# FFN1's first pair: another order of its operands, copies and second-half products

## The chip, the cores and the metric

The kernel runs on one core of a Trainium2 chip. Its time is the device time of one execution in microseconds (us). Three runs of the kernel before took 1942.91, 1944.48 and 1946.78 us; their median is 1944.48.

The engines are called as in the profile: PE is TensorE (matrix products; PEld its weight loads), DVE is VectorE, ACT is ScalarE, POOL is GpSimd, and SP is the engine that issues most DMA transfers. Each has its own queue of instructions; they meet at semaphores.

## What is computed

One layer of a decoder over 1048 tokens (16 meta tokens, 1024 of a prompt, 8 of samples), width 1024, in float32. The layer has a half-step FFN, a mixer with two kinds of recurrent heads, and a second half-step FFN:

```
def rmsnorm(x, w):
    xf = x.astype(jnp.float32)
    y = xf * lax.rsqrt(jnp.mean(xf * xf, axis=-1, keepdims=True) + EPS)
    return (y * w.astype(jnp.float32)).astype(x.dtype)

def swiglu(x, wg, wu, wd):
    return (jax.nn.silu(x @ wg) * (x @ wu)) @ wd
...
    h = h + 0.5 * swiglu(rmsnorm(h, n1), w1g, w1u, w1d)
...
    h = h + mix
    h = h + 0.5 * swiglu(rmsnorm(h, n2), w2g, w2u, w2d)
```

The change lies in the first line of the layer, in the first 60 of some 1940 us: the start of `x @ wg` and `x @ wu` of FFN1, whose hidden width is 2816.

## The kernel before

**Products.** The activations stand transposed: features on the 128 partitions, tokens along the row. The tokens are cut into two halves of 524 (c = 0 and 1) and each half into two quarters of 262 (Q). For each block of 128 hidden columns f, `pair` makes gate and up values together by a scheme with seven products in place of eight: the weights are seen as a 2 x 2 matrix (gate or up, first or second 512 features), the activations of a half as another (first or second 512 features, first or second quarter). Operands 1, 7, 2 and 3 (activations) and 1, 7, 4 and 2 (weights) are plain blocks, the others are sums and differences of them: for the activations 5 = 7 - 1, 6 = 3 - 5, 7 becomes 3 - 7, and 4 = 2 - 6. Product p multiplies weight operand p by activation operand p. Products 2, 3 and 4 are added into the PSUM banks of 1, 5 and 7.

**Two parts.** Float32 operands are split in a high part (a cast on ACT, `cast` at L348 for activations, `hi` at L464 for weights) and a low part (the difference, on DVE, `low` at L354 and `lo` at L468). Sums of activations are made on DVE at L343, sums of weights at L460. `mm3` (L163 to L165) makes each product out of three matmuls: high by high, high by low part of the activations, low part of the weights by high. A product over 512 features is 12 matmuls of 262 columns; its first needs the casts, its second the activations' low part, its third the weights' low part.

**Order by hand.** An FFN is one list of steps, `Steps`; a step is a product and what is done after it (`post`). `S.before(i, fn)` puts other work ahead of step i. The queues of PE, DVE, ACT and SP follow the order of the code (`manual_schedule`), so the lists of `before(...)` in `first1` are these engines' queues, read per engine.

**The first pair.** For f = 0 the two halves are multiplied one after the other, since the input is still arriving. Steps 0 to 5 are the first half's products in the order that `first1` returns (1, 2, 5, 6, 7, 3), steps 6 to 11 the second half's in the same order, steps 12 and 13 operand 4 of the first and of the second half. Step 14 begins the next pair, f = 1, whose own weights are planned by `Left.plan` from step 3 on (loads at steps 3 and 4, sums at 10 to 12, the first cast at 11, its low part at 12). In `first1`, `o` is the first half's set of operands, `e` the second half's, `w` the weights. So "e.low 6" is the low part of the second half's operand 6, "o.sum_4" the first half's sum 4, "w.lo 4" the low part of weight operand 4. Ahead of step 0 the first half is transposed and operands 1 and 2 are made.

**The input.** The second half's tokens come in by `place_k`: for each of the 8 blocks k of 128 features, PE makes four transposes (L1191) into one PSUM bank, and ACT takes from it two scaled copies (L1193, one per quarter, times the norm's weight) into the operands' blocks and two raw copies (L1194) into blocks that SP stores to DRAM (`x.store`, L1216) for the residual. Blocks 0 to 3 are the first 512 features (operands 1 and 7), 4 to 7 the second (2 and 3). `tail` places the last 12 tokens, with a multiply on DVE (L1178) and raw copies on ACT. `x.square` (L1210) squares the raw input for the norm's root, which is needed only at step 18. The operands and raw blocks share 30 SBUF buffers called "u"; four PSUM banks ("mis") serve the transposes, and two of them are held by product 7 and operand 4 of each half.

**After a product.** After product 1 ACT copies its bank to z (L676), and product 2 may write into that bank only then; after product 2 ACT copies the sum out (L680). After products 6, 7, 3 and 4 DVE adds into SBUF (L678 and L685, L687, L691, L705); what belongs to product 5 waits for 6.

Of the kernel before, what the change touches and what calls it, by code (L numbers as in the profile page):

```python
# [17 lines left out]
P = 128  # L18
# [10 lines left out]
Q = T // 4  # L29
# [38 lines left out]
class Core:  # L68
# [49 lines left out]
    def raw(self, w=512):  # L118
        t = self.tmp.tile([P, 512], F32, tag="r", name=self.uid("r"), bufs=8)
        return t[:, :w]  # L120
# [530 lines left out]
def pair(K, S, wg, wu, f, ops, spread, hid, late_r, first=None, inner=None):  # L651
# [70 lines left out]
    if inner:  # L722
# [34 lines left out]
        e = len(S.steps)  # L757
# [12 lines left out]
    late = {}  # L770
# [9 lines left out]

    order = first(S, left)
    unit = Unit(K, left.w, [o.op for o in ops], 4, post_first)
    for ps_ in (order[:6], order[6:]):
        for c in range(2):
            for p in ps_:
                unit.step(S, p, c, (c,), True)
    cs = slice(0, 2)
    for i, (fn, *args) in enumerate(((silu, 0, cs), (silu, 1, cs), (times_r, "u0", 0, cs), (product_, 0, cs), (times_r, "u1", 1, cs), (product_, 1, cs))):
# [342 lines left out]
class Input:  # L1131
# [51 lines left out]

        return scaled, raw

    def place_k(self, k):

        K = self.K
        ps = K.psm()
        for i in range(4):  # L1190
            K.nc.tensor.transpose(ps[:, i * P : i * P + P], self.x[5 + i][:, k * P : k * P + P], K.ident)  # L1191
        for q, c0, c1 in ((2, 0, Q), (3, Q, 4 * P)):
            K.nc.scalar.activation(self.block(k // 4, q)[:, k % 4, : c1 - c0], ps[:, c0:c1], AF.Identity, scale=self.wcol[:, k : k + 1])  # L1193
            K.nc.scalar.copy(self.raw_block(k // 4, q)[:, k % 4, : c1 - c0], ps[:, c0:c1])  # L1194

    def block(self, b, q):
        o = self.ops[q // 2]
# [877 lines left out]
def body(ctx, tc, a, o):  # L2075
    nc = tc.nc
    K = Core(ctx, tc)
# [6 lines left out]
    x = Input(K, a, wn1, ops, spread)  # L2084

    def before(S, i, *fns):
        for fn in fns:
            S.before(i, (lambda fn=fn: fn[0](*fn[1:])))

    def first1(S, w):  # L2090
        o, e = ops
        x.load(0, 1, 2)
        K.keep_clock(14)
        w.load(1)
        x.load(3, 4)
        for p in (2, 7, 4):
            w.load(p)
        x.load(*range(5, 10))
        nc.scalar.preload_act_table_set("sqrt_and_others")
        columns1()  # L2100
        for i in range(2):
            scaled, raw = x.place(i)
            K.keep_clock(4)
            for fn in (scaled, raw):
                fn(0)
                fn(1)
        w.hi(1)
        scaled, raw2 = x.place(2)
        K.keep_clock(4)
        scaled(0)  # L2110
        o.cast(1)
        scaled(1)
        raw2(0)
        raw2(1)
        scaled, raw3 = x.place(3)
        K.keep_clock(4)
        scaled(0)
        o.low(1)
        scaled(1)
        w.lo(1)  # L2120
        w.hi(2)
        o.cast(2)
        scaled, raw4 = x.place(4)
        K.keep_clock(4)
        scaled(0)
        scaled(1)
        raw3(0)
        raw3(1)
        raw4(0)
        raw4(1)  # L2130
        x.square(4)
        o.low(2)
        w.lo(2)
        o.sum_(5)

        def tail():
            scaled, raw = x.place(9)
            for fn in (scaled, raw):
                fn(0)
                fn(1)  # L2140

        before(S, 1, (o.cast, 5), (w.sum_, 5), (w.hi, 5), (o.sum_, 6), (x.store, 0), (columns,), (x.place_k, 0))
        before(S, 2, (o.low, 5), (o.cast, 6), (w.lo, 5), (w.sum_, 6), (w.hi, 6), (x.place_k, 1))
        before(S, 3, (o.low, 6), (o.sum_, 7), (w.lo, 6), (o.cast, 7), (w.sum_, 7), (w.sum_, 3), (w.hi, 7), (x.place_k, 2))
        before(S, 4, (o.low, 7), (w.lo, 7), (o.cast, 3), (w.hi, 3), (x.place_k, 3), (tail,))
        before(S, 5, (o.low, 3), (w.lo, 3), (e.cast, 1), (e.sum_, 5), (x.store, 1, (0,)), (x.place_k, 4), (x.place_k, 5))
        before(S, 6, (e.low, 1), (e.cast, 5), (o.sum_, 4), (x.place_k, 6), (x.place_k, 7))
        before(S, 7, (e.cast, 2), (e.low, 5), (e.low, 2), (e.sum_, 6), (x.store, 1, (1,)), (o.cast, 4), (e.cast, 6))
        before(S, 8, (o.low, 4), (e.sum_, 7), (e.low, 6), (e.cast, 7))
        before(S, 9, (e.sum_, 4), (e.low, 7), (e.cast, 3), (x.square, 9))  # L2150
        before(S, 10, (e.low, 3), (e.cast, 4), (w.hi, 4), (w.lo, 4), (x.square, 0), (x.square, 1))
        before(S, 11, (e.low, 4), (x.square, 2))
        for i, n in enumerate((3, 5, 6, 7, 8)):
            before(S, 12 + i, (x.square, n))
        before(S, 18, (x.rms,))
        before(S, 22, *((x.spread_r, q) for q in range(4)))
        return 1, 2, 5, 6, 7, 3, 4

    def from1(o):
        return x.d[o * P : (o + 1) * P, :]  # L2160
# [1 line left out]
    def after1(S, h, e3, e0, e1):  # L2162
# [33 lines left out]
        return nm.add  # L2196

    ffn(K, a["w_ffn1_gate"][0], a["w_ffn1_up"][0], a["w_ffn1_down"][0], ops, spread, from1, first1, after1, 26)

    constants_mix(K, a)  # L2200
# [15 lines left out]
    order = "q0 f0 v0 g0 q1 f1 v1 g1 z0 q2 f2 v2 g2 q3 f3 v3 z1 g3".split()  # L2216
    raw = ("q0", "f0", "g0", "q1", "g3")
# [3 lines left out]
    with K.tc.manual_schedule(engines={mybir.EngineType.PE}):  # L2221
# [33 lines left out]
        late = late_norms(K, pieces, lambda: us[3]["g"], fill)  # L2255
# [48 lines left out]
    def first2(S, w):  # L2304
        o, e = ops2
        for p in (1, 7, 4, 2):
            w.load(p)
        o.scaled(h, wn2, (1, 7))
        o.cast(1)
        o.sum_(5)  # L2310
        o.scaled(h, wn2, (2, 3))
        o.cast(5)
        o.low(1)
        o.cast(2)
        o.sum_(6)
        o.low(5)
        o.cast(6)
        o.low(2)
        o.sum_(7)
        o.cast(7)  # L2320
        o.low(6)
        o.sum_(4)
        o.cast(3)
        o.low(7)
        o.cast(4)
        o.low(3)
        o.low(4)
        for p in (5, 6, 7, 3):
            w.sum_(p)
        w.split(1)  # L2330
        w.split(5)
        e.scaled(h, wn2, (1, 7))
        e.cast(1)
        e.sum_(5)
        e.low(1)
        e.cast(5)
        w.split(6)
        e.low(5)
        e.scaled(h, wn2, (2,), (0, 1))
        w.split(2)  # L2340
        e.scaled(h, wn2, (2,), (2,))
        before(S, 1, (e.scaled, h, wn2, (2,), (3,)), (w.hi, 7), (e.scaled, h, wn2, (3,), (0, 1)), (w.lo, 7))
        before(S, 2, (w.hi, 3), (e.scaled, h, wn2, (3,), (2, 3)), (e.cast, 2))
        before(S, 3, (w.lo, 3), (e.sum_, 6), (e.low, 2), (nf2.begin_half, 1))
        before(S, 4, (e.cast, 6), (e.sum_, 7))
        before(S, 5, (e.low, 6), (e.cast, 7))
        before(S, 6, (e.low, 7), (e.sum_, 4))
        before(S, 7, (e.cast, 3))
        before(S, 8, (e.cast, 4))
        before(S, 9, (e.low, 3), (w.hi, 4))  # L2350
        before(S, 10, (w.lo, 4), (e.low, 4), (keep2, 1))
        before(S, 15, (nf2.finish, (1, 1)))
        return 1, 5, 6, 2, 7, 3, 4

    def after3(S, h, e3, e0, e1):
        nf = []
# [15 lines left out]
        return None  # L2372

    ffn(K, a["w_ffn2_gate"][0], a["w_ffn2_up"][0], a["w_ffn2_down"][0], ops2, spread2, lambda o: hd2[o], first2, after3, 14)


# [35 lines left out]
```

## Time and profile before

| | us |
|---|---|
| runs (median of three) | 1944.48 |
| the profiled execution | 1946.32 |
| its span, first to last instruction | 1944.5 |
| busy in the span: DVE | 1535.0 |
| busy in the span: ACT | 847.1 |
| busy in the span: POOL | 92.3 |

The mean granted clock of TensorE over the span is 0.995 of full speed. A row of the order in time reads: start (us from the start of the span), length, engine, line, operation, out <- in with partitions x columns and types, count, and in square brackets the idle time of that engine just before, with the work that ended it. A row of the groups by line reads: line, engine, operation, out <- in, shapes, count, then busy time in us and mean ns of one, then idle time before them and what ended most of it. A row of stretches gives from:to, its length, then the busy time of PE, PEld, DVE, ACT and POOL with the number of instructions, the granted clock of TensorE (1 is full), the mean busy share of the 16 DMA engines, and GB/s. Neighbouring instructions of a kind that run without a gap are merged in one row. A result is finished a little after the next instruction of its engine has started, so a queue's pace is read from start to start and a dependence from the end.

### The profile page before, as it was taken

To read this page: it belongs to the slowest core of one execution; us is meant where nothing else is said; L and a number is where in the kernel's file an instruction comes from. 1 tells how busy PE (TensorE), PEld (TensorE's weight loads), DVE (VectorE), ACT (ScalarE), POOL (GpSimd) and SP (SyncE) were. 2 spreads that over 40 slices of the span, in tenths; PEclk is the share of its full clock that TensorE was granted. 3 is DMA by queue.
4 is the path that set the end of the run, shared out by engine and by line. 5 is a ranking of instruction groups with operands and counts; after the bars stand their busy time and mean duration, and the time that the engine had idled before them with its cause. 6 is when DMAs were issued, how large, how long until landed. Compare 5 with 4: busy or idle time off the path is not lost.

```text
span 1944.5 us, 41083 instructions
## 1 busy us (share of the span) xinstructions
PE 1912.5 (98%) x16571; PEld 1881.1 (97%) x16571; DVE 1535.0 (79%) x2802; ACT 847.1 (44%) x1639; POOL 92.3 (5%) x155
## 2 busy tenths in 40 slices
PE   7999999999999999999999999999999999999998
PEld 6999999999999999999999989999999999999998
DVE  7788888888788877576765657898888888878965
ACT  7623232233533644476543545752232333354353
POOL 4000000000000410000000001200000000000000
PEclk9999999999999999999999999999999999999999
DMA  7233233335978551231642354233233333587862
GB/s 223 77 89 110 90 103 105 95 104 163 274 230 264 161 162 44 60 101 29 183 131 66 104 182 143 72 100 114 83 109 94 108 100 109 161 239 238 277 186 78
DMA packets 324646, 260.59 MB, mean 134 GB/s; under 512 B 17824, under 2 KB 299680, under 8 KB 324448
## 3 DMA queue, kind: packets, MB, share of 16 engines
q1 hardware_dynamic: 324216, 257.92, 43.7%
q8 instruction: 131, 2.15, 0.5%
q14 instruction: 59, 0.48, 0.1%
q0 software_dynamic: 224, 0.04, 0.0%
q10 hardware_dynamic: 16, 0.00, 0.0%
HBM read 192.90 MB, written 65.07 MB: 133 GB/s over the span
## 4 chain that ended last, share of the span: by engine, by line
PE 92%; DVE 4%; DMA 1%; issue 1%; ACT 1%; SPq 0%; DVEq 0%; POOL 0%; ACTq 0%; POOLq 0%
PE acc L163 27%; PE acc L165 27%; PE acc L164 27%; PE mis L163 2%; PE mis L165 2%; PE mis L164 2%; DMA s<-in_x_prompt_dram 1%; PE mis L1809 1%; PE mis L1457 0%; PE mis L1880 0%; PE mis L1453 0%; DVE u L354 0%; PE mis L1785 0%; DVE t L303 0%; PE mis L1448 0%
## 5 line engine op out<-in xcount | busy, mean ns | idle before, releaser
L163 PE MATMUL acc<-u,ws 128*128 128x258 f32 (+4 forms) x4226 | 1235.1, 293 | 3.0 <-ACT u L348 1.4
L164 PE MATMUL acc<-u,ws 128*128 128x258 f32 (+4 forms) x4226 | 1224.4, 290 | 3.6 <-DVE u L354 3.3
L165 PE MATMUL acc<-u,ws 128*128 128x258 f32 (+4 forms) x4226 | 1224.9, 290 | 2.9 <-DVE ws L468 2.7
L164 PEld LDWEIGHTS acc<-u,ws 128*128 128x128 f32 x4226 | 801.1, 190 | 7.4 <-DVE u L354 4.4
L163 PEld LDWEIGHTS acc<-u,ws 128*128 128x128 f32 x4226 | 799.5, 189 | 6.4 <-issue 1.7
L165 PEld LDWEIGHTS acc<-u,ws 128*128 128x128 f32 x4226 | 798.1, 189 | 4.4 <-DVE ws L468 4.0
L468 DVE TENSOR_TENSOR ws<-r,ws 128x512 fp32r<-128x512 f32 x276 | 190.3, 690 | 74.6 <-ACT ws L464 74.5
L464 ACT CAST ws<-r 128x512 fp32r<-128x512 f32 x276 | 160.0, 614 | 13.1 <-ACT ws L464 7.8
L460 DVE TENSOR_TENSOR r<-r,r 128x512 f32<-128x512 f32 x176 | 121.5, 692 | 2.8 <-DMA r<-in_w_ffn_up_dram 1.3
L683 ACT ACTIVATE t<-t 128x516 f32<-128x516 f32 (+1 forms) x41 | 26.2, 639 | 210.8 <-DVE t L671 210.8
L714 ACT ACTIVATE t<-t 128x524 f32<-128x524 f32 (+1 forms) x47 | 30.0, 639 | 197.9 <-DVE t L671 197.9
L851 DVE TENSOR_TENSOR u<-u,u 128x1048 fp32r<-128x1048 f32 (+3 forms) x84 | 97.1, 1157 | 5.5 <-ACT u L847 5.5
L671 DVE TENSOR_TENSOR t<-t,u 128x524 f32<-128x524 f32 (+1 forms) x135 | 93.1, 697 | 2.8
L232 POOL TENSOR_TENSOR t<-t,t 128x262 f32<-128x262 f32 (+1 forms) x56 | 54.7, 986 | 798.7 <-ACT t L231 795.4
L158 DVE TENSOR_TENSOR ws<-r,ws 128x512 fp32r<-128x512 f32 x88 | 60.8, 703 | 36.8 <-ACT ws L157 36.6
L908 ACT CAST ws<-u 128x512 fp32r<-128x512 f32 (+1 forms) x72 | 42.1, 585 | 102.0 <-DVE u L903 96.4
L847 ACT CAST u<-u 128x1048 fp32r<-128x1048 f32 (+3 forms) x84 | 82.8, 988 | 0.0
L908 ACT CAST ws<-r 128x512 fp32r<-128x512 f32 (+1 forms) x84 | 47.9, 582 | 71.6 <-DVE r L903 38.4
L937 DVE SCALAR_TENSOR_TENSOR s<-acc,s 128x524 f32<-128x524 f32 (+3 forms) x86 | 53.8, 649 | 29.4 <-PE acc L165 29.1
L913 DVE TENSOR_TENSOR ws<-r,ws 128x512 fp32r<-128x512 f32 (+1 forms) x84 | 57.5, 694 | 24.0 <-ACT ws L908 23.9
L157 ACT CAST ws<-r 128x512 fp32r<-128x512 f32 x88 | 54.0, 618 | 39.7 <-PE acc L165 34.0
L913 DVE TENSOR_TENSOR ws<-u,ws 128x512 fp32r<-128x512 f32 (+1 forms) x72 | 46.8, 650 | 26.5 <-ACT ws L908 26.5
(444 smaller groups left out, 2327.5 us busy)
## 6 DMA issues: line engine op xcount, KB each, us to landing
r<-in_w_ffn_down_dram SPq DMA_DIRECT2D x128, 256.0 KB
hd<-s SPq DMA_DIRECT2D x93, 258.0 KB
r<-in_w_ffn_gate_dram SPq DMA_DIRECT2D x88, 256.0 KB
r<-in_w_ffn_up_dram SPq DMA_DIRECT2D x88, 256.0 KB
hd<-s SPq DMA_DIRECT2D x77, 262.0 KB
u<-hd SPq DMA_DIRECT2D x36, 516.0 KB
u<-hd SPq DMA_DIRECT2D x28, 524.0 KB
r<-in_w_in_dram SPq DMA_DIRECT2D x56, 256.0 KB
```

The lines of the kernel that those rows point to most:

```text
L158: self.nc.vector.tensor_sub(lo, src, hi.bitcast(F32))
L163: mm(ps, whi, xhi, start=first, stop=False, skip_group_check=more)
L164: mm(ps, whi, xlo, start=False, stop=False, skip_group_check=more)
L165: mm(ps, wlo, xhi, start=False, stop=last, skip_group_check=more)
L460: self.K.nc.vector.tensor_tensor(self.raw[p], self.raw[x], self.raw[y], op)
L464: self.K.nc.scalar.copy(self.w[p][:, : self.n * P], self.raw[p])
L468: self.K.nc.vector.tensor_sub(t[:, 512 : 512 + w], self.raw[p], t[:, :w].bitcast(F32))
L671: nc.vector.tensor_mul(t, t if src is None else src, spread.lanes(i, cs))
L847: K.nc.scalar.copy(hi, lo.bitcast(F32))
L851: K.nc.vector.tensor_sub(lo, lo.bitcast(F32), hi.bitcast(F32))
L908: nc.scalar.copy(w[p, j, g][:, : n * P], src)
L913: nc.vector.tensor_sub(t[:, 512 : 512 + n * P], box[0], t[:, : n * P].bitcast(F32))
```

## The change

Three things change, all in the order of the first pair; no instruction is added or left out.

- `first1` returns one order for each half: the first half as before, the second as 1, 5, 2, 6, 7, 3. (FFN2's `first2` returns its old order twice and is as before.)
- `place_k` can put off its two raw copies; for blocks 6 and 7 they come after the cast of the second half's operand 2.
- the lists ahead of steps 3 to 12 are dealt out anew: w.lo 6 ahead of o.sum_7; w.sum_3 one step later; e.cast 1, e.low 1 and e.cast 5 one step earlier, e.cast 5 thereby ahead of `place_k` 4 and 5; the first half's operand 4 (sum, cast, low part and its weights) from steps 6 to 10 to steps 9 to 11; the second half's sum 7 behind low part 6, and so on; the squares one or two steps later.

```
-    for ps_ in (order[:6], order[6:]):
+    for ps_ in (order, [(4,)] * 2):
         for c in range(2):
-            for p in ps_:
+            for p in ps_[c]:
                 unit.step(S, p, c, (c,), True)
...
-    def place_k(self, k):
+    def place_k(self, k, late=False):
 
         K = self.K
         ps = K.psm()
         for i in range(4):
             K.nc.tensor.transpose(ps[:, i * P : i * P + P], self.x[5 + i][:, k * P : k * P + P], K.ident)
-        for q, c0, c1 in ((2, 0, Q), (3, Q, 4 * P)):
+        qs = (2, 0, Q), (3, Q, 4 * P)
+
+        def raw(q, c0, c1):
+            K.nc.scalar.copy(self.raw_block(k // 4, q)[:, k % 4, : c1 - c0], ps[:, c0:c1])
+
+        for q, c0, c1 in qs:
             K.nc.scalar.activation(self.block(k // 4, q)[:, k % 4, : c1 - c0], ps[:, c0:c1], AF.Identity, scale=self.wcol[:, k : k + 1])
-            K.nc.scalar.copy(self.raw_block(k // 4, q)[:, k % 4, : c1 - c0], ps[:, c0:c1])
+            if not late:
+                raw(q, c0, c1)
+        return lambda: [raw(*q) for q in qs]
...
-        before(S, 3, (o.low, 6), (o.sum_, 7), (w.lo, 6), (o.cast, 7), (w.sum_, 7), (w.sum_, 3), (w.hi, 7), (x.place_k, 2))
-        before(S, 4, (o.low, 7), (w.lo, 7), (o.cast, 3), (w.hi, 3), (x.place_k, 3), (tail,))
-        before(S, 5, (o.low, 3), (w.lo, 3), (e.cast, 1), (e.sum_, 5), (x.store, 1, (0,)), (x.place_k, 4), (x.place_k, 5))
-        before(S, 6, (e.low, 1), (e.cast, 5), (o.sum_, 4), (x.place_k, 6), (x.place_k, 7))
-        before(S, 7, (e.cast, 2), (e.low, 5), (e.low, 2), (e.sum_, 6), (x.store, 1, (1,)), (o.cast, 4), (e.cast, 6))
-        before(S, 8, (o.low, 4), (e.sum_, 7), (e.low, 6), (e.cast, 7))
-        before(S, 9, (e.sum_, 4), (e.low, 7), (e.cast, 3), (x.square, 9))
-        before(S, 10, (e.low, 3), (e.cast, 4), (w.hi, 4), (w.lo, 4), (x.square, 0), (x.square, 1))
-        before(S, 11, (e.low, 4), (x.square, 2))
+        raws = []
+
+        def place_late(k):
+            raws.append(x.place_k(k, True))
+
+        def raw_late():
+            for fn in raws:
+                fn()
+
+        before(S, 3, (o.low, 6), (w.lo, 6), (o.sum_, 7), (o.cast, 7), (w.sum_, 7), (w.hi, 7), (x.place_k, 2))
+        before(S, 4, (o.low, 7), (w.lo, 7), (o.cast, 3), (w.sum_, 3), (w.hi, 3), (x.place_k, 3), (tail,), (e.cast, 1))
+        before(S, 5, (o.low, 3), (w.lo, 3), (e.sum_, 5), (e.low, 1), (e.cast, 5), (x.store, 1, (0,)), (x.place_k, 4), (x.place_k, 5))
+        before(S, 6, (e.low, 5), (place_late, 6), (place_late, 7), (e.cast, 2), (raw_late,))
+        before(S, 7, (e.low, 2), (e.sum_, 6), (e.cast, 6), (x.store, 1, (1,)))
+        before(S, 8, (e.low, 6), (e.sum_, 7), (e.cast, 7))
+        before(S, 9, (e.low, 7), (e.cast, 3), (o.sum_, 4))
+        before(S, 10, (e.low, 3), (o.cast, 4), (w.hi, 4), (e.sum_, 4))
+        before(S, 11, (o.low, 4), (w.lo, 4), (e.cast, 4), (x.square, 9), (x.square, 0))
+        before(S, 12, (e.low, 4), (x.square, 1), (x.square, 2))
...
-        return 1, 2, 5, 6, 7, 3, 4
+        return (1, 2, 5, 6, 7, 3), (1, 5, 2, 6, 7, 3)
...
-        return 1, 5, 6, 2, 7, 3, 4
+        return ((1, 5, 6, 2, 7, 3),) * 2
```

## The prediction, made before the changed kernel was run

> **What bounds the kernel now.** I read the page first, then the run cut into stretches of 5 us, then the three engines in order of time around FFN1's first pair.
>
> ```profile
> span 1944.5 us, 41083 instructions
> PE 1912.5 (98%) x16571; PEld 1881.1 (97%) x16571; DVE 1535.0 (79%) x2802; ACT 847.1 (44%) x1639; POOL 92.3 (5%) x155
> 20.00:25.00 5.00, 4.69 (x28) 4.48 (x26) 4.36 (x6) 3.65 (x10) 4.67 (x7) 0.68 1.10 276
> 30.00:35.00 5.00, 4.70 (x23) 4.30 (x24) 2.98 (x6) 3.92 (x12) 0.00 (x0) 0.66 0.64 216
> 40.00:45.00 5.00, 3.31 (x25) 3.11 (x25) 4.24 (x5) 3.05 (x4) 0.00 (x0) 1.00 0.59 197
> 45.00:50.00 5.00, 2.96 (x23) 2.54 (x21) 4.97 (x7) 3.15 (x5) 0.00 (x0) 1.00 0.00 0
> ```
>
> TensorE is busy 98% of the span, so the whole kernel can only move where TensorE waits. The first pair is such a place: in 40 to 50 us it is busy 6.27 of 10 us, and VectorE 9.21. (Column order: stretch, length, busy time of PE, weight loads, DVE, ACT, POOL, granted clock, DMA share, GB/s.) POOL is empty here. What TensorE waited for between 36 and 58 us (the second half and the seam to the next pair), grouped by line, and five of its rows in order of time:
>
> ```profile
> L164 PE MATMUL acc<-u,ws 128*128 128x262 f32 x23 | 7.0, 302 | 3.3 <-DVE u L354 3.3
> L163 PE MATMUL acc<-u,ws 128*128 128x262 f32 x23 | 6.7, 293 | 1.4 <-ACT u L348 1.4
> L165 PE MATMUL acc<-u,ws 128*128 128x262 f32 x23 | 6.6, 289 | 0.3 <-DVE ws L468 0.3
> L164 PE MATMUL mis<-u,ws 128*128 128x262 f32 x12 | 3.6, 301 | 1.4 <-DVE u L354 1.4
> ```
>
> ```profile
> 42.08 0.40 PE L164 MATMUL acc<-u,ws 128*128 128x262 f32 x1 [0.90 <-DVE u L354]
> ...
> 55.11 0.39 PE L164 MATMUL mis<-u,ws 128*128 128x262 f32 x1 [0.77 <-DVE u L354]
> ...
> 56.56 0.28 PE L163 MATMUL acc<-u,ws 128*128 128x262 f32 x1
> 56.68 0.28 PE L164 MATMUL acc<-u,ws 128*128 128x262 f32 x1
> 57.26 0.39 PE L165 MATMUL acc<-u,ws 128*128 128x262 f32 x1 [0.29 <-DVE ws L468]
> ```
>
> The idle columns add to 6.4 us; nothing in this pair can win more. 2.3 of it stand at product 2 (1.4 of L163 and the 0.90 at 42.08), 0.77 at the second half's operand 4 (55.11), 0.29 at the next pair's weights (57.26), the rest at products 1, 6, 7 and 3. Who ends them is VectorE at L354 (the low parts), and VectorE's own row of work between 40.77 and 57 us shows why:
>
> ```profile
> 24.89 0.68 DVE L468 TENSOR_TENSOR ws<-r,ws 128x512 fp32r<-128x512 f32 x1
> ...
> 30.63 0.32 DVE L1178 TENSOR_TENSOR u<-mis,col 128x48 f32<-128x48 f32 x2 [0.83 <-ACT u L1193]
> ...
> 34.45 1.24 DVE L343 TENSOR_TENSOR u<-u,u 128x1048 f32<-128x1048 f32 x1
> ...
> 37.61 1.24 DVE L343 TENSOR_TENSOR u<-u,u 128x1048 f32<-128x1048 f32 x1
> ...
> 40.77 1.25 DVE L354 TENSOR_TENSOR u<-u,u 128x1048 fp32r<-128x1048 f32 x1 [0.76 <-ACT u L348]
> ...
> 49.71 1.24 DVE L354 TENSOR_TENSOR u<-u,u 128x1048 fp32r<-128x1048 f32 x1
> 51.54 0.69 DVE L468 TENSOR_TENSOR ws<-r,ws 128x512 fp32r<-128x512 f32 x1 [0.59 <-ACT ws L464]
> 52.15 1.41 DVE L460 TENSOR_TENSOR r<-r,r 128x512 f32<-128x512 f32 x2
> ...
> 53.82 1.24 DVE L354 TENSOR_TENSOR u<-u,u 128x1048 fp32r<-128x1048 f32 x1
> 54.98 0.68 DVE L460 TENSOR_TENSOR r<-r,r 128x512 f32<-128x512 f32 x1
> 55.58 0.42 DVE L691 TENSOR_TENSOR t<-acc,t 128x262 f32<-128x262 f32 x1
> ...
> 56.52 0.68 DVE L468 TENSOR_TENSOR ws<-r,ws 128x512 fp32r<-128x512 f32 x1
> ```
>
> From 40.77 to 57.2 VectorE stands still once, 0.59 us. A large subtraction (L343 a sum, L354 a low part) takes 1.16 us from start to next start and is finished 1.24 us after its start. **So VectorE's queue sets when the pair ends, and every idle moment that a new order puts into this queue is paid at the end.** The rows stand in the order of the code, step by step: at 51.54 the weights' low part waits for its cast while two sums that need nothing (52.15) wait behind it.
>
> **The change, part by part.** Nothing is added or removed: the same 7 products, sums, casts and copies are issued in another order on PE, DVE and ACT. I therefore walk the two queues with the durations above and these of ScalarE:
>
> ```profile
> 25.00 1.06 ACT L348 CAST u<-u 128x1048 fp32r<-128x1048 f32 x1 [0.72 <-DVE u L343]
> ...
> 31.25 1.08 ACT L348 CAST u<-u 128x1048 fp32r<-128x1048 f32 x1
> 33.20 0.48 ACT L1193 ACTIVATE u<-mis,col 128x262 f32<-128x262 f32 x1 [0.87 <-PE mis L1191]
> 33.58 0.37 ACT L1194 COPY u<-mis 128x262 f32<-128x262 f32 x1
> 33.83 0.48 ACT L1193 ACTIVATE u<-mis,col 128x250 f32<-128x250 f32 x1
> ...
> 34.44 0.51 ACT L1193 ACTIVATE u<-mis,col 128x262 f32<-128x262 f32 x1
> ...
> 39.67 2.03 ACT L348 CAST u<-u 128x1048 fp32r<-128x1048 f32 x2
> 43.22 1.07 ACT L348 CAST u<-u 128x1048 fp32r<-128x1048 f32 x1 [1.51 <-DVE u L343]
> ```
>
> One step of transposed copies (place_k) holds ScalarE 1.24 us (33.20 to 34.44): two scaled copies of 0.37 (33.20 to 33.58) and two raw ones of 0.26 (33.58 to 33.83), so 0.74 where the raw ones are put off. A cast holds it about 0.97 and is done after 1.07.
>
> *Up to step 4.* w.lo 6 (24.89) goes ahead of o.sum_7: it is done 1.16 us sooner, and o.sum_7 0.60 later, at 25.5. ScalarE's cast of operand 7 (25.00) thus begins at 25.56 and the queue behind it runs 0.3 to 0.4 us late, since w.hi 3 now also waits for w.sum_3, which is moved behind w.lo 7. The tail's multiply (30.63) comes at 31.0. TensorE's products 6 and 7 of the first half end about 1 us earlier; nobody waits for them at that point.
>
> *Steps 5 and 6: the wait that I think decides.* e.cast 5 is moved ahead of place_k 4 and 5. It needs e.sum_5, and VectorE reaches that after the tail, post 7, o.low 3 and w.lo 3: 31.0 + 0.35 + 0.35 + 1.16 + 0.60 = 33.4, done 34.65 (before: 34.45 to 35.69). ScalarE is through with e.cast 1 (31.25 before, now 31.65) by 32.6 and now stands about 2.1 us, with place_k 4 to 7 behind it. From 34.7: cast 0.97, two whole place_k 2.5, two half ones 1.48, and e.cast 2 begins at 39.65. Before it began at 39.67. **The moved raw copies save ScalarE 1.05 us here and the new wait eats them: e.low 2 starts at 40.8 in both kernels.** Product 5 now fills TensorE from 38.9 to 40.4, where it stood still; product 2 follows at 42.1, since the copy of product 1's bank has moved behind four raw copies (39.65 + 0.97 + 1.05, done 42.05). At 43.6 TensorE is about 1.4 us ahead of before.
>
> *Steps 7 to 12.* VectorE's row from the start of e.low 2 to that of e.low 4, before: 53.82 - 40.77 = 13.05 us. What the new order adds:
> - o.sum_4 stood at 37.61, before e.low 2, and now comes behind e.low 7, where VectorE has no idle time to give: +1.16. The time that it leaves free becomes idle (37.3 to 40.8).
> - o.low 4 stood between e.sum_6 and e.low 6 and covered e.cast 6. Now e.low 6 follows e.sum_6 directly and waits: cast 1.07 + two hand-overs of 0.04 + the 0.08 by which a result trails the next start = +1.23.
> - e.sum_7 now stands behind e.low 6, and e.low 7 behind e.sum_7; e.sum_4 no longer lies between. e.cast 7 can begin only after e.sum_7: the same wait again, +1.23.
> - the next pair's sum_7 and the addition after product 3 now stand ahead of e.low 4: 0.60 + 0.34 = +0.94.
> - w.lo 4 no longer waits for w.hi 4, which is done long before: 51.54 less (49.71 + 1.16) = -0.67.
>
> Sum +3.89: e.low 4 starts at 57.7, ends at 58.95, and TensorE's last product goes on at 59.0 instead of 55.11. By then the next pair's weights are ready (57.7 + 1.16 + 0.60 + 0.68 = 60.1, for a matmul at 60.7), so the wait at 57.26 falls away: from 55.11 an unbroken row would have reached that matmul at 56.80 (56.68 and a spacing of 0.12, as from 56.56), so -0.46. **Net +3.43 us.** On the way TensorE waits at 45.6 (product 6), 49.2 (7), 52.3 (3) and 56.3 and 56.9 (the first half's 4): all inside the 59.0.
>
> *After it.* ScalarE's nine squares take 1.05 each:
>
> ```profile
> L1210 ACT ACTIVATE s<-s 128x1024 f32<-128x1024 f32 x6 | 6.3, 1049 | 0.0
> ```
>
> They come later, but the root needs them only with step 18, some 6 us after the next pair begins. Between them stand the casts of that pair's weights: e.cast 4 at 53.45, six squares and a cast put the second one at 61.2, its low part at 62.6; TensorE asks for it after two products of 1.47, at 63.4. I cost both at nothing: TensorE's own work covers them, by 0.8 us; if that cover were gone, about 1 us.
>
> *Queues of SP.* The stores of the raw blocks wait for the deferred copies, and one weight load for w.lo 4, 4.6 us later than here:
>
> ```profile
> 30.25 9.50 SPq L1216 DMA_DIRECT2D xT<-u  x4
> 52.26 0.37 SPq L454 DMA_DIRECT2D r<-in_w_ffn_gate_dram  x1
> ```
>
> That load is first read at about 69 us (+3.4); at nothing. Behind the stores nothing else is due before it.
>
> *The clock.* In 20 to 25 and 30 to 35 us the granted clock is 0.68 and 0.66, each after a stretch in which TensorE had hardly run.
>
> ```profile
> 20.46 0.42 PE L164 MATMUL acc<-u,ws 128*128 128x262 f32 x1
> 20.68 0.42 PE L165 MATMUL acc<-u,ws 128*128 128x262 f32 x1
> ```
>
> Here matmuls start 0.22 us apart, elsewhere 0.12. The low stretch of 30 to 33 us delays ScalarE before the change (0.87 idle at 33.20, a wait for transposes), but not after it, where ScalarE waits for VectorE then: an execution without it would have a faster kernel before by up to 0.87, and the change would cost that more. The changed kernel has its own hole, 53.7 to 56.9 us, where TensorE runs one matmul; a low stretch right behind it would spread some 11 matmuls by 0.10 = 1.1 us. Neither comes in every execution; bounds 0 and 2.0, I take 0.9, about half. [...]
>
> **Sum:** 3.43 + 0.9 = +4.3 us. The profiled execution has a span of 1944.5 and took 1946.32, 1.8 above the median 1944.48; the difference is carried over to the median: 1948.8 us (+0.22%).
>
> **Rivals.**
> 1. *ScalarE is let go early.* If the wait for e.sum_5 is short, because the tail's multiply doesn't wait for place_k 3, e.cast 2 starts up to 2.1 us earlier and everything behind it: 3.43 - 2.1 = +1.3, 1945.8 to 1946.7 with the clock. For it: VectorE has 1.7 us free before the tail. Against: row 30.63 shows exactly this wait (0.83, for ScalarE).
> 2. *Not slower: the engines pass over what waits.* If VectorE could run e.sum_7 while e.low 6 waits, and o.sum_4 in the hole at 37 us, 2.46 + 1.16 of the 3.43 are gone: -0.2, 1944.3; with the waits at product 2 gone too (2.3), 1942. It decides at the instruction behind e.low 6. Against: 51.54, where two free sums waited behind. [...]
> 3. *A transfer joins in.* The second block's raw copies end at 41.8 instead of 39.4, so its two stores, which filled 40 to 45 us (197 GB/s), land near 45.7. If e.low 6 (44.3) takes over a buffer of theirs it waits 1.4 more: +5.7, 1950.2. Against: by my count two of the 30 buffers are free then.
>
> **Numbers.** The walk as forecast (+3.4 to +5.4): 0.65; rival 1: 0.15; rival 2: 0.08; rival 3: 0.12. What a measurement can tell from no change is 0.2%, 3.9 us. Faster by more: most of 6.4 us would have to be won, 0.05 (out of rival 2). Within: rival 1, the rest of rival 2 and the lower quarter of the forecast, 0.15 + 0.03 + 0.16 = 0.34. Slower: 0.61. Range 1945.4 to 1950.8: from below rival 1 with no clock part to above rival 3; the forecast alone 1947.9 to 1949.9.
>
> **What would show it.** In the changed trace: a wait of ScalarE of about 2 us for L343 near 33 to 35 us, ahead of the transposed copies; e.low 2 at 40.8 after 3.5 us of idle VectorE; two waits of 1.2 us of L354 for L348 near 43 and 47 us; no TensorE wait between products 1 and 5; the next pair's start at 60.5 instead of 56.56; all later stages moved alike. I am wrong if e.low 2 starts before 39, if either of the two waits is missing, or if a later stage takes the 3.4 us back.

## The result, and the profile after

| | before | after |
|---|---|---|
| median of six runs each | 1944.78 | 1951.13 us (1949.16 to 1952.40) |
| ratio of the two, 95% interval | | 1.0035 [1.0024, 1.0045] |
| the profiled execution | 1946.32 | 1951.44 |
| its span | 1944.5 | 1949.7 |

The change makes the kernel slower by 6.35 us. The forecast was +4.3 and the range ended at 1950.8, so the direction was right and the size was 2 us short. Of the runs further below, e1_fill and e2_cast5 had one execution each at a low mean granted clock (0.65 and 0.75; 2625.89 and 2300.57 us); their medians are those of the other eleven.

In the changed kernel's code some lines have new numbers: L1198 is the scaled copy (L1193 before), L1195 the raw copy (L1194), L1217 the square (L1210). The page's head, and two of the stretches of 5 us (columns as in the prediction):

```profile
span 1949.7 us, 41079 instructions
PE 1913.6 (98%) x16571; PEld 1881.1 (96%) x16571; DVE 1535.6 (79%) x2802; ACT 849.1 (44%) x1639; POOL 88.6 (5%) x155
...
30.00:35.00 5.00, 4.55 (x21) 4.04 (x21) 3.28 (x7) 4.23 (x10) 0.00 (x0) 0.66 0.56 176
...
45.00:50.00 5.00, 3.02 (x19) 2.23 (x17) 2.79 (x3) 2.52 (x4) 0.00 (x0) 1.00 0.50 166
```

The busy times are those of before: the same work. In 45 to 50 us TensorE and VectorE are now *both* idle for about 2 of 5 us; before, VectorE had no such room. VectorE's own rows in order of time say why:

```profile
24.25 1.25 DVE L354 TENSOR_TENSOR u<-u,u 128x1048 fp32r<-128x1048 f32 x1 [1.17 <-ACT u L348]
...
32.73 0.32 DVE L1178 TENSOR_TENSOR u<-mis,col 128x48 f32<-128x48 f32 x2 [1.70 <-ACT u L1198]
...
42.54 1.25 DVE L354 TENSOR_TENSOR u<-u,u 128x1048 fp32r<-128x1048 f32 x1 [3.46 <-ACT u L348]
43.70 1.24 DVE L343 TENSOR_TENSOR u<-u,u 128x1048 f32<-128x1048 f32 x1
46.08 1.25 DVE L354 TENSOR_TENSOR u<-u,u 128x1048 fp32r<-128x1048 f32 x1 [1.13 <-ACT u L348]
47.25 1.24 DVE L343 TENSOR_TENSOR u<-u,u 128x1048 f32<-128x1048 f32 x1
49.63 1.25 DVE L354 TENSOR_TENSOR u<-u,u 128x1048 fp32r<-128x1048 f32 x1 [1.13 <-ACT u L348]
50.91 1.25 DVE L343 TENSOR_TENSOR u<-u,u 128x1048 f32<-128x1048 f32 x1
...
52.88 1.24 DVE L354 TENSOR_TENSOR u<-u,u 128x1048 fp32r<-128x1048 f32 x1
54.16 1.25 DVE L343 TENSOR_TENSOR u<-u,u 128x1048 f32<-128x1048 f32 x1
...
58.15 0.68 DVE L468 TENSOR_TENSOR ws<-r,ws 128x512 fp32r<-128x512 f32 x1
...
59.69 1.24 DVE L354 TENSOR_TENSOR u<-u,u 128x1048 fp32r<-128x1048 f32 x1
```

Read by names: o.low 6 (24.25), the tail (32.73), e.low 2 (42.54), e.sum_6, e.low 6, e.sum_7, e.low 7, o.sum_4, e.low 3, e.sum_4, w.lo 4 and e.low 4 (59.69). Each low part of the second half's operands 6 and 7 follows its own sum directly and stands 1.13 us until ScalarE has cast that sum. ScalarE's rows show the two casts, and the new wait ahead of them:

```profile
36.45 1.07 ACT L348 CAST u<-u 128x1048 fp32r<-128x1048 f32 x1 [2.02 <-DVE u L343]
37.43 0.47 ACT L1198 ACTIVATE u<-mis,col 128x262 f32<-128x262 f32 x1
...
41.35 1.15 ACT L348 CAST u<-u 128x1048 fp32r<-128x1048 f32 x1
...
43.37 0.52 ACT L676 COPY t<-acc 128x262 f32<-128x262 f32 x1
44.98 1.07 ACT L348 CAST u<-u 128x1048 fp32r<-128x1048 f32 x1 [1.10 <-DVE u L343]
48.53 1.07 ACT L348 CAST u<-u 128x1048 fp32r<-128x1048 f32 x1 [2.48 <-DVE u L343]
```

At 36.45 e.cast 5 has waited 2.02 us for e.sum_5, and block 4's copies (37.43) stood behind it; e.cast 2 comes at 41.35, e.low 2 after it. TensorE's waits:

```profile
38.85 0.66 PE L1191 MATMUL mis<-ident,s 128*128 128x128 f32 x4 [1.62 <-ACT u L1195]
...
43.93 0.40 PE L163 MATMUL acc<-u,ws 128*128 128x262 f32 x1 [1.50 <-ACT t L676]
...
58.29 0.39 PE L164 MATMUL mis<-u,ws 128*128 128x262 f32 x1 [2.38 <-DVE u L354]
...
60.99 0.39 PE L164 MATMUL mis<-u,ws 128*128 128x262 f32 x1 [0.48 <-DVE u L354]
...
62.43 0.28 PE L163 MATMUL acc<-u,ws 128*128 128x262 f32 x1
...
62.80 0.29 PE L163 MATMUL acc<-u,ws 128*128 128x262 f32 x1
```

The idle time that stood at product 2 for its low part is gone; the largest wait is now 2.38 us at the first half's operand 4 (58.29), and the next pair (62.43) begins without one.

**Where the time of this one execution went.** I cut each trace at two points: T0, the start of o.low 6, behind which VectorE's order differs; and T1, the next pair's fourth matmul. Before: 22.51 and 57.48. After: 24.25 and 62.80. So 1.74 us are lost ahead of T0, +3.58 between, and behind T1 the two differ by 0.12 (1887.02 and 1886.90 to the end of the span). The 1.74 isn't the change's: both kernels issue the same work in the same order up to there, and another profile of the same changed kernel (r1_after below) has T0 at 22.54. The +3.58 is the predicted 3.43; it isn't 6.35. That difference is what the second and third set of experiments are about.

### The profile page after: what moved, and what is told of

It reads as the page before. It is cut to its first block, busy times and chain, and to the rows that moved or that the text cites. A ratio compares the mean times of both kernels' runs of the same rounds, so it can differ in the third digit from the quotient of the medians.

```text
span 1949.7 us, 41079 instructions
## 1 busy us (share of the span) xinstructions
PE 1913.6 (98%) x16571; PEld 1881.1 (96%) x16571; DVE 1535.6 (79%) x2802; ACT 849.1 (44%) x1639; POOL 88.6 (5%) x155
## 4 chain that ended last, share of the span: by engine, by line
PE 89%; DVE 7%; DMA 1%; ACT 1%; issue 1%; SPq 0%; DVEq 0%; POOL 0%; ACTq 0%; POOLq 0%
PE acc L163 26%; PE acc L165 26%; PE acc L164 26%; PE mis L163 2%; PE mis L164 2%; PE mis L165 2%; DVE u L851 1%; DMA s<-in_x_prompt_dram 1%; DVE ws L913 1%; PE mis L1816 1%; PE mis L1464 0%; DVE u L354 0%; DVE s L937 0%; PE mis L1887 0%; PE mis L1460 0%
## 5 line engine op out<-in xcount | busy, mean ns | idle before, releaser
L908 ACT CAST ws<-r 128x512 fp32r<-128x512 f32 (+1 forms) x84 | 48.0, 584 | 71.1 <-DVE r L903 37.1
```

The lines of the kernel that those rows point to most:

```text
L908: nc.scalar.copy(w[p, j, g][:, : n * P], src)
```

## The experiments

All medians are in us, with the ratio to the kernel before, measured beside it on the same chip; its medians were 1944.99 in the first set, 1943.98 in the second and 1944.55 in the third (34 or 35 executions each). T0 to T1 and the low stretch (a stretch of the first pair in which the granted clock is 0.50) are those of the one profiled execution of each.

| run | median | ratio, 95% | T0 to T1 | low stretch, us |
|---|---|---|---|---|
| e1_fill | 1945.44 | 0.9998 [0.9989, 1.0008] | 35.41 | 47.8 to 54.6 |
| e2_cast5 | 1947.94 | 1.0014 [1.0005, 1.0024] | 37.70 | 56.5 to 59.9, two early ones |
| e3_both | 1942.75 | 0.9993 [0.9984, 1.0001] | 32.21 | 46.3 to 49.8, two early ones |
| e4_order | 1944.09 | 0.9995 [0.9987, 1.0004] | 34.03 | 44.2 to 51.0 |
| r1_after | 1951.30 | 1.0033 [1.0023, 1.0044] | 38.48 | none |
| r2_before | 1945.51 | 1.0004 [0.9994, 1.0015] | 34.02 | 42.4 to 45.8 |
| r3_after_clock | 1948.02 | 1.0019 [1.0009, 1.0030] | 39.21 | 50.3 to 60.5 |
| r4_before_clock | 1942.63 | 0.9993 [0.9982, 1.0003] | 34.01 | 39.9 to 46.7 |
| h1_after_hold | 1946.44 | 1.0010 [1.0001, 1.0018] | 38.46 | 33.7 to 37.1 |
| h2_before_hold | 1942.13 | 0.9988 [0.9980, 0.9997] | 33.96 | none |
| h3_both_hold | 1943.13 | 0.9994 [0.9985, 1.0003] | 32.81 | 33.1 to 36.5 |
| e5_swap | 1948.04 | 1.0018 [1.0007, 1.0028] | 37.28 | 27.8 to 31.2, 55.1 to 58.5 |

### First set: the parts of the order

**e1_fill** is the changed kernel with the order of before behind e.low 2, so that another instruction stands between each sum and its low part:

```
-        before(S, 7, (e.low, 2), (e.sum_, 6), (e.cast, 6), (x.store, 1, (1,)))
-        before(S, 8, (e.low, 6), (e.sum_, 7), (e.cast, 7))
-        before(S, 9, (e.low, 7), (e.cast, 3), (o.sum_, 4))
...
+        before(S, 7, (e.low, 2), (e.sum_, 6), (o.cast, 4), (e.cast, 6), (x.store, 1, (1,)))
+        before(S, 8, (o.low, 4), (e.sum_, 7), (e.low, 6), (e.cast, 7))
+        before(S, 9, (e.sum_, 4), (e.low, 7), (e.cast, 3))
```

with o.sum_4 ahead of `place_late` 6 and steps 10 to 12 following suit.

> The changed kernel with only the order behind e.low 2 put back: o.sum_4 again ahead of e.low 2 (in VectorE's hole), o.low 4 between e.sum_6 and e.low 6, e.sum_7 ahead of e.low 6, e.sum_4 ahead of e.low 7, e.low 4 ahead of the next pair's sum 7. The product order, the moved e.cast 5 and the late raw copies stay. The walk of VectorE's queue: o.sum_4 (1.16), the two waits (1.13 each) and 0.94 of others fall away, about 4.2 us less than the changed kernel, so near 1947, and e.low 2 still starts some 3.5 us after e.low 5 has ended save for the one sum. Rival, the loss is ScalarE's wait for e.sum_5: that stays, so at most 1.2 us less, near 1950. Rival, product 2 waits for the copy of product 1's bank: that stays too, near 1951.

**e2_cast5** is the changed kernel with e.cast 5 moved back behind `place_k` 4 and 5 (from ahead of them in the list for step 5 to the head of step 6's). **e3_both** does both, with o.sum_4 one place earlier than in e1_fill, ahead of e.low 5. **e4_order** is the kernel before with the second half's products 1, 5, 2 alone and nothing else of the change.

> The changed kernel with only e.cast 5 put back behind place_k 4 and 5. The walk: ScalarE's wait for e.sum_5 (2.0 us) falls away, e.cast 2 and all behind it come about 2 us earlier, the two waits of VectorE for e.cast 6 and e.cast 7 stay: about 2 us less than the changed kernel, near 1949. Rival, ScalarE's wait is the whole loss: back to the kernel before, near 1945. Rival, the loss is in the clock or in the arrival of the input: no change, near 1951.

> Both edits of the two runs beside it, on the changed kernel: e.cast 5 behind place_k 4 and 5, and the order behind e.low 2 put back. The walk: the two savings add, about 6 us less than the changed kernel, near 1945, level with the kernel before or up to 1.5 us faster (e.low 2 near 39 us from an equal start instead of 40.8). Rival, the two parts hide one another: no better than the better of the two alone, near 1947.

> The kernel before with only the second half's product order 1, 5, 2, nothing else. The walk: products 5 and 2 trade places, product 6 still waits for e.low 6, which VectorE's queue sets: no change, within 0.5 us of the kernel before. Rival, the order of the products is what costs: product 2's end and its copy on ScalarE come later, 2 us or more slower.

VectorE's rows of e1_fill, e.low 2 first, e.low 4 last:

```profile
40.29 1.25 DVE L354 TENSOR_TENSOR u<-u,u 128x1048 fp32r<-128x1048 f32 x1 [2.29 <-ACT u L348]
41.46 1.25 DVE L343 TENSOR_TENSOR u<-u,u 128x1048 f32<-128x1048 f32 x1
42.63 1.25 DVE L354 TENSOR_TENSOR u<-u,u 128x1048 fp32r<-128x1048 f32 x1
...
52.67 1.24 DVE L354 TENSOR_TENSOR u<-u,u 128x1048 fp32r<-128x1048 f32 x1
```

and of e2_cast5, the same two:

```profile
38.70 1.25 DVE L354 TENSOR_TENSOR u<-u,u 128x1048 fp32r<-128x1048 f32 x1 [1.17 <-ACT u L348]
...
55.86 1.24 DVE L354 TENSOR_TENSOR u<-u,u 128x1048 fp32r<-128x1048 f32 x1
```

In e1_fill no low part waits any more, and the row from e.low 2 to e.low 4 takes 12.38 us (52.67 less 40.29) in place of 17.15 (59.69 less 42.54). In e2_cast5 that row is as long as in the changed kernel (17.16), but it begins 16.23 us after T0 in place of 18.29: 2.06 us earlier, the whole of the wait at e.cast 5. The two faults are independent and each stands where the prediction put it: e3_both has both savings in full (e.low 2 begins 16.17 us after T0, and e.low 4 starts 12.37 behind e.low 2). In the medians they are worth some 5.7 us (1951.13 to 1945.44) and 3.2 us (to 1947.94); with both mended the kernel stands at 1942.75, 2.2 under the kernel before beside it, with an interval that still reaches 1. The product order as such does nothing (e4_order).

Both gains in the median are larger than in the rows (4.77 and 2.06), but not by more than the noise: the kernel before alone has medians from 1943.98 to 1945.51 (r2_before). e1_fill and e3_both came out 1.6 and 2.2 us under what was expected of them.

### Second set: the clock early in the pair

Both kernels were repeated as they are (r1_after, r2_before) and with 26 matmuls added whose results are overwritten, 16 ahead of block 0's transposes and 10 ahead of block 3's, so that no low stretch falls at 20 or 30 us (r3_after_clock, r4_before_clock):

```
         for i in range(4):
+            if i == 0:
+                for _ in range(K.hold.get(k, 0)):
+                    wt, xt = K.holds()
+                    K.nc.tensor.matmul(ps[:, :Q], wt, xt, start=True, stop=True)
             K.nc.tensor.transpose(ps[:, i * P : i * P + P], self.x[5 + i][:, k * P : k * P + P], K.ident)
...
+        K.hold = {0: 16, 3: 10}
+        K.holds = lambda: (w.w[1][:, :P], o.op[1][0][:, :Q])
```

> The changed kernel once more, for its time beside the kernel before on one chip and for a second profile. The walk: from the start of o.low 6 to the next pair's fourth matmul 38.5 us as in the first profile (34.97 before), so 3.6 us slower plus what the clock adds, ratio 1.0018 to 1.0030. Rival, something else than this pair's queues adds to it: again 6 us or more, ratio 1.0030 or higher, with the excess outside that stretch.

> The kernel before once more, for a second profile. Clock theory: where no low stretch lies at 30 us, the stretch from o.low 6 to the next pair's fourth matmul takes some 0.9 us less than the 34.97 of the first profile; where it lies there again, the same. Rival, the stretch is fixed by the queues alone: 34.97 within 0.2 in any case. Its time is level with the other runs of the kernel before.

> The changed kernel with 26 extra matmuls into banks that the transposes overwrite (16 ahead of block 0's, 10 ahead of block 3's), in time in which TensorE waits, so that it looks busy around 17 and 28 us. Clock theory: no low stretch at 20 and 30 us, but ScalarE waits for VectorE all the same: at most 0.5 us faster than the changed kernel. Rival, the low clock at 30 us costs the changed kernel too: 1 us or more faster.

> The kernel before with the same 26 extra matmuls. Clock theory: no low stretch at 20 and 30 us, place_k 4 is no longer late: 0.5 to 1.4 us faster than the kernel before, so that the distance between the two kernels with extra matmuls is 4.5 us or more. Rival, the clock takes from both alike: the distance stays at the walk's 3.4 to 3.6.

With no low stretch at 30 us the kernel before takes 34.0 us from T0 to T1 in place of 34.97 (34.02, 34.01 and, in e4_order, 34.03), and the changed one 38.48, the same as its 38.55 with one. The prediction's 0.87 was right and is 0.95: the order of before suffers from that stretch (e.low 2 begins 18.26 us after T0 with it and 17.31 without, in r2_before), the changed one is waiting for VectorE then. So **the queues alone cost 4.46 us** (38.48 less 34.02).

r1_after's own expectation held for T0 to T1 and not for the time: its ratio of 1.0033 is above the 1.0018 to 1.0030 that was expected, and in the range of its rival, an excess outside that stretch.

The expectation for r3_after_clock was a miss. The 26 matmuls took 3.3 us off the changed kernel, not half a microsecond, although its T0 to T1 got no shorter; its one profile doesn't show where. It shows where the clock was low instead, in stretches of 3.4 us (PE's busy time is the second number, its instructions stand behind it, and the granted clock is the third from the end):

```profile
43.50:46.90 3.40, 2.05 (x14) 1.65 (x14) 2.41 (x2) 0.92 (x2) 0.00 (x0) 1.00 0.63 216
46.90:50.30 3.40, 1.86 (x13) 1.45 (x12) 2.45 (x3) 2.12 (x3) 0.00 (x0) 1.00 0.00 0
50.30:53.70 3.40, 2.58 (x11) 2.00 (x10) 3.33 (x6) 1.61 (x3) 0.00 (x0) 0.50 0.00 0
...
57.10:60.50 3.40, 3.40 (x15) 3.40 (x16) 3.40 (x6) 3.40 (x8) 0.00 (x0) 0.50 0.27 77
```

Ahead of the low stretch TensorE had 13 matmuls at work in 3.4 us, where some 28 fit at a spacing of 0.12; the clock came back only behind a stretch in which it was busy throughout (57.1 to 60.5). Inside T0 to T1 these 10.2 us cost only 0.73 (39.21 less 38.48), since TensorE was waiting anyway. The stretches of 5 us of r1_after, which happened to have no low clock, show how thin that part of the changed kernel is:

```profile
40.00:45.00 5.00, 2.75 (x19) 2.13 (x17) 3.12 (x3) 3.15 (x7) 0.00 (x0) 1.00 0.49 168
45.00:50.00 5.00, 2.86 (x19) 2.45 (x20) 3.83 (x4) 2.31 (x3) 0.00 (x0) 1.00 0.14 46
50.00:55.00 5.00, 2.84 (x20) 2.25 (x18) 4.90 (x8) 2.89 (x4) 0.00 (x0) 1.00 0.00 0
55.00:60.00 5.00, 2.79 (x18) 2.38 (x19) 5.00 (x8) 5.00 (x10) 0.00 (x0) 1.00 0.19 52
```

That also bears on a rival that I held then, that the 2 us were lost in some later stage: behind T1 the four profiles of the changed order average 1885.3 us and the five of before's order 1885.0, while single ones of one order lie up to 4 us apart. No such loss shows, but with so few and so scattered a loss of 2 us isn't excluded by them alone. Low stretches there, in all profiles, are single ones of 3.4 us between 760 and 1130 us and one at the very end, and the changed order has no more of the single ones than the other (1, 1, 0 and 2 against 2, 1, 1, 1 and 1).

### Third set: the holes filled, and one swap

h1_after_hold and h2_before_hold also put matmuls into the thin places behind 36 us, ahead of steps of the list (8 to 13: 10, 10, 12, 12, 20, 4 in the changed order; 6, 7, 9, 10, 13: 4, 16, 10, 4, 4 in that of before), 94 and 64 in all; h3_both_hold does it to e3_both (16, 10, 4 and 4 ahead of steps 7, 9, 10 and 13, not the numbers that its expectation gives).

```
+        def hold(n):
+            ps = K.psm()
+            for _ in range(n):
+                K.nc.tensor.matmul(ps[:, :Q], w.w[3][:, :P], o.op[1][0][:, :Q], start=True, stop=True)
```

> The changed kernel with extra matmuls in every hole of TensorE in the first pair: the 26 of the run before, and 10, 10, 12, 12, 20 and 4 ahead of the second half's products 2, 6, 7, 3 and of the two products 4, into a spare bank. Clock theory: no low stretch between 14 and 62 us, the stretch from o.low 6 to the next pair's fourth matmul stays near 38.5, the executions lie closer together and some 4 us under the changed kernel, near 1947; the distance to the kernel before with the same means is the queues' alone, 4.5 us. Rival, the 2 us above the queues' loss have another cause: no more than 0.5 us faster than with the 26 alone (1948.0).

> The kernel before with extra matmuls in its holes: the 26, and 4, 16, 10, 4 and 4 ahead of the second half's products 1, 2, 6, 7 and 4. Clock theory: no low stretch between 14 and 60 us, o.low 6 to the next pair's fourth matmul 34.0 us, near 1942.5, 1.5 to 2.5 us faster than the kernel before. Rival: level with the kernel before.

> The kernel of e.cast 5 behind place_k 4 and 5 and the old order behind e.low 2, with extra matmuls in its holes (26, and 10, 10, 12, 20 and 4 ahead of the products 6, 7, 3 and the two products 4). Clock theory and the walk add: o.low 6 to the next pair's fourth matmul near 32.2, near 1941 and 3 us faster than the kernel before. Rival, the extra matmuls delay products that are now ready sooner: no faster than without them (1942.7).

Two of the same stretches of h1_after_hold:

```profile
45.00:50.00 5.00, 4.22 (x33) 3.87 (x32) 3.83 (x4) 2.31 (x3) 0.00 (x0) 1.00 0.13 44
...
55.00:60.00 5.00, 4.79 (x36) 4.18 (x34) 5.00 (x8) 5.00 (x10) 0.00 (x0) 1.00 0.19 52
```

TensorE is kept busy where it stood, and T0 to T1 is unchanged (38.46 and 33.96): the added matmuls cost the queues nothing. (One low stretch is left, at 33.7 us, where none was expected.) Yet the changed kernel falls by 4.9 us, from 1951.30 to 1946.44 (on another chip, on which the kernel before is 0.6 us slower), and the one before by 1.9 to 2.4 (from 1944.0 or 1944.55, that set's own, to 1942.13). What is left between the two orders is 4.31 us: the 4.46 of the queues, within what twelve executions of each can tell (about 1.3 us at a spread of 1.6). **So of the measured difference up to 4.46 us are queue time, and the rest, 1.9 us in the first measurement (6.35) and 2.9 in r1_after's (1951.30 less 1943.98), goes when TensorE is kept busy.** Nothing reads what the added matmuls make, which points to TensorE's clock (its mean is 0.9950 in r1_after and 0.9976 in h1_after_hold). The size of that rest is uncertain, since the intervals of both measurements begin at 1.0024 and 1.0023, some 4.5 us, hardly above the queues' share; and no profile shows the whole of it. h2_before_hold, the order of before with its holes filled, is the only kernel here whose whole interval is faster than before.

h3_both_hold is a miss: it was to reach 1941 and took no less than e3_both without the filling (1943.13 and 1942.75). Why filling doesn't help that order isn't settled; its profile has a low stretch at 33.1 to 36.5 us, outside the places that I filled, and e.low 2 begins 16.77 us after T0 in it in place of e3_both's 16.17. The mean granted clock rose there too, from 0.9958 to 0.9975, and the time didn't fall: a higher mean clock alone was no gain here.

**e5_swap** tests the cheapest repair, two neighbours of the changed kernel exchanged:

```
-        before(S, 8, (e.low, 6), (e.sum_, 7), (e.cast, 7))
+        before(S, 8, (e.sum_, 7), (e.low, 6), (e.cast, 7))
```

> The changed kernel with two instructions traded: e.sum_7 ahead of e.low 6. The walk: e.sum_7 covers e.cast 6 and e.low 6 covers e.cast 7, so both waits of VectorE (1.13 each) go: e.low 2 to e.low 4 takes 14.8 us instead of 17.15, and the kernel is 2.3 us faster than the changed one, near 1949. Rival, the waits move to the next place in the queue (e.cast 3 or the first half's operand 4): less than 1 us, near 1951.

```profile
39.88 1.25 DVE L354 TENSOR_TENSOR u<-u,u 128x1048 fp32r<-128x1048 f32 x1 [3.45 <-ACT u L348]
41.05 2.40 DVE L343 TENSOR_TENSOR u<-u,u 128x1048 f32<-128x1048 f32 x2
43.43 2.41 DVE L354 TENSOR_TENSOR u<-u,u 128x1048 fp32r<-128x1048 f32 x2
...
54.65 1.24 DVE L354 TENSOR_TENSOR u<-u,u 128x1048 fp32r<-128x1048 f32 x1
```

Two sums in a row, then two low parts in a row: while VectorE makes the second sum, ScalarE casts the first, and both waits are gone with one exchange. From e.low 2 to e.low 4 it is 14.77 us in place of 17.15, so 2.38 less. The median falls by 3.1 to 3.3 (from 1951.13 and 1951.30 to 1948.04).

## Why the prediction was right, and where it was wrong

- **The wait of e.cast 5 for e.sum_5: right.** Said 2.1 us, measured 2.02; e.low 2 was to begin at the same time in both, and begins 18.26 us after T0 before and 18.29 after. e2_cast5 proves it: without the wait, 16.23. Rival 1 (ScalarE let go early) falls with it; the tail waited for block 3's copies, as said (32.73, 1.70 idle).
- **The walk from e.low 2 to e.low 4: right.** Said +3.89, measured +4.10 (17.15 less 13.05). Each of the two waits was to cost 1.23 over the usual 1.16 from start to start; the rows give 2.38 less 1.16 = 1.22. The 0.21 over is in two sums (50.91, 54.16) that begin 1.28 behind the low part ahead, when that is finished, and not 1.16; why stays open.
- **The seam to the next pair: right.** Said -0.46; e.low 4 to T1 takes 3.11 after and 3.66 before, -0.55.
- **Rival 2 (engines pass over waits): no.** e.sum_7 (47.25), which needed nothing of e.low 6, stood behind its wait of 1.13 us. **Rival 3 (a transfer joins in): no;** none of the waits quoted ends on a DMA, and e.low 6's wait is the cast's alone.
- **Not foreseen, and free:** block 7's transposes waited 1.62 us for a PSUM bank (38.85), until block 4's raw copies were done, which ScalarE's wait at e.cast 5 had held up; in e2_cast5, without that wait, both blocks are transposed in one go. Product 5 still ended by 42.4, ahead of the z copy at 43.37 that product 2 needed.
- **The failed step is the clock term**, "bounds 0 and 2.0, I take 0.9, about half". Beside the walk's 3.43 the measured difference leaves 2.9 (6.35 less 3.43), more than the upper bound. Its first part, up to 0.87 where a low stretch at 30 us hurts only the kernel before, was right in kind and is 0.95. Its second part, estimated at 11 matmuls and 1.1 us where a low stretch comes behind the hole, was right in size for one stretch: from e.low 4 to T1 it takes 3.11 or 3.12 us in the changed kernel, r1_after and h1_after_hold, which have no low stretch there, and 3.86, 4.24 and 4.31 in r3_after_clock, e5_swap and e2_cast5, which have one, so 0.75 to 1.2 more. The order of before had low stretches between 40 and 51 us in r2_before, r4_before_clock and e4_order and lost nothing by them (34.02, 34.01 and 34.03, against 33.96 without).
- **What stood behind the step** is that it asked for a hole in which TensorE does next to nothing, found one, and halved the cost for chance. In its words both low stretches of the first trace came "after a stretch in which TensorE had hardly run". That holds for the first (1.31 of 3.41 us busy); ahead of the second TensorE was busy 2.40 us, with twelve small transposes among its instructions (the row below). By that row no empty stretch was needed, and the changed kernel is thin from 40 to 60 us (2.75 to 2.86 busy of each 5 in r1_after): in the changed order and its variants a low stretch began at 46.3 (e3_both), 47.8 (e1_fill), 50.3 (r3_after_clock), 55.1 (e5_swap) or 56.5 us (e2_cast5) and lasted 3.4 to 10.2. Taken in full, what the profiles show is the walk's 3.58, 0.95 and up to 1.2: 5.7 us, inside the measured interval. The last 0.6 of the 6.35 is in no profile, and its cause stays open.

```profile
26.58:29.99 3.41, 2.40 (x20) 1.81 (x19) 2.81 (x5) 3.41 (x9) 0.25 (x1) 1.00 0.68 188
```

What one low stretch costs is seen in e1_fill, where it falls on dense work. Two neighbours of TensorE at a granted clock of 0.50, and two right behind it:

```profile
51.14 0.42 PE L163 MATMUL acc<-u,ws 128*128 128x262 f32 x1
51.36 0.42 PE L164 MATMUL acc<-u,ws 128*128 128x262 f32 x1
...
54.76 0.28 PE L165 MATMUL mis<-u,ws 128*128 128x262 f32 x1
54.88 0.29 PE L163 MATMUL mis<-u,ws 128*128 128x262 f32 x1
```

The first are 0.22 us apart, the second 0.12. From 48.95 to 54.63 us that cost 26 matmuls 0.10 each, 2.6 us, of which some 1.1 reached T1: from e.low 4 (52.67) to T1 (57.45) it takes 4.78 us, and 3.67 in e3_both, which has the same order there and its clock back by then. That the changed kernel loses more in the same way, by low stretches that reach past 60 us into the dense next pair, fits but isn't shown: none of the four profiles of its order caught one there, and of the timed executions only the mean clock is known. It averages 0.9950 for r1_after, 0.9957 for the kernel before beside it, and 0.9976 and 0.9977 for the two filled ones. A thousandth of the time is 1.9 us, so r1_after lacks 1.4 us of full clock more than the kernel before: of the size of the rest, and no proof of where.

## What to carry to other kernels

Where one engine makes a value, a second casts it and the first reads the cast, put another instruction of the first engine between: VectorE ran nothing past its two waits of 1.13 us here, and exchanging two neighbours was worth 2.4 us in the queue and about 3 in the time. An early consumer at the head of a queue held up all that stood behind it (e.cast 5, 2.02 us). Walk a changed order instruction by instruction against the durations of the trace; it came out within 0.2 us. Then add TensorE's clock: an order that thins out TensorE over 20 us can pay beside its waits where a low stretch reaches dense work (some 1.1 us up to T1 in e1_fill), and filling such places with matmuls that nothing reads gave 5 us back to the changed order and 2 to the one before (to none in a third order), without hurting the queues.

## What the hardware showed that was not expected

**Half clock without a long gap.** Ahead of r3_after_clock's low stretch no wait was longer than 0.9 us: from 46.9 to 50.3 us eleven matmuls started, and TensorE waited twice (0.64 and 0.90). Ahead of e1_fill's twelve had started:

```profile
44.40:47.80 3.40, 1.54 (x12) 1.52 (x12) 3.40 (x4) 1.75 (x3) 0.00 (x0) 1.00 0.25 83
47.80:51.20 3.40, 2.83 (x14) 2.63 (x13) 3.37 (x6) 3.31 (x6) 0.00 (x0) 0.50 0.00 0
```

In e2_cast5 a stretch as thin kept its clock, and only the one behind it was followed by the half clock:

```profile
49.66:53.08 3.42, 1.73 (x12) 1.52 (x12) 3.35 (x5) 1.71 (x3) 0.00 (x0) 1.00 0.00 0
53.08:56.49 3.41, 1.82 (x12) 1.58 (x12) 3.41 (x6) 3.41 (x8) 0.00 (x0) 1.00 0.05 14
56.49:59.90 3.41, 2.94 (x14) 2.75 (x13) 2.16 (x4) 3.41 (x8) 0.00 (x0) 0.50 0.28 83
59.90:63.31 3.41, 3.41 (x30) 3.41 (x29) 1.71 (x3) 3.02 (x7) 0.00 (x0) 1.00 0.45 131
```

In the profiles' record of the clock each low stretch of the first pair lasts 3.4, 6.8 or 10.2 us, and the rows above are cut at that length. A hole in which TensorE does next to nothing, as the prediction had it, is too narrow: here stretches in which TensorE was busy about half of the time (1.54 to 1.86 of 3.4 us) were followed by the half clock, though not always (1.73 in e2_cast5; 1.6 to 2.2 in every such stretch of the changed kernel from 37 to 61 us, and no low stretch). The half clock stayed through stretches with 2.26, 2.58 and 2.83 us busy and ended behind ones with 2.94 and 3.40. What decides between them these few don't show. In these three runs thin work was dear twice: the clock fell to 0.50 behind it, and came back to 1.00 only behind a stretch of nearly dense work (2.94 or 3.40 us) that had been run at 0.50.

**The place is chance.** r1_after has the same order as the changed kernel and the same holes, and no low stretch in the pair; the kernel before had its own at 20 and 30 us or at 42. That profile is of the fastest of r1_after's twelve executions (1948.43, with a median of 1951.30). The timed executions of r1_after and of the kernel before spread with a standard deviation of 2.2 and 2.3 us, those of the two filled kernels with 1.6; but e3_both, e4_order and e5_swap, which aren't filled, have 1.7, so the spread alone tells little. A single profile doesn't show what such a kernel loses in the mean.
